# A fourth buffer for the scores of a top-16 retrieval, paid for from two other buffers

## The chip, the cores and the metric

The kernel runs on one core of a Trainium2 chip. The metric is the time of one execution on the device, in microseconds. Engines are named as in the profile: PE is TensorE (PEld its weight loads), DVE VectorE, ACT ScalarE, POOL GpSimd, SP SyncE, which issues most of the DMAs.

## What is computed

One layer of a hybrid of parallel branches, for a prompt of 1024 rows and a sample group of 64 rows that share all weights (D is 1024), in float32:

```
xn = rmsnorm(x);  p = xn @ w_in + b_in
x += (sum over 3 branches of sigmoid(gate) * branch(xn)) @ w_out     # mLSTM, spatial gating, cross-attention
xn = rmsnorm(x)                                                      # then the PEER experts:
q  = xn @ w_pq                                    # 8 heads x 256
s1, s2 = q[..., :128] @ k_sub1.T, q[..., 128:] @ k_sub2.T            # 128 scores each
(v1, i1), (v2, i2) = top16(s1), top16(s2)
cand = v1[:, None] + v2[None, :]                  # 16 x 16 candidates, again the top 16 of them
e, g = expert numbers, softmax of their scores    # 8 x 16 = 128 experts a row
a    = gelu(sum(u_exp[e] * xn));  x += sum((g * a) * v_exp[e])
y = rmsnorm(x)
```

There are 16384 experts. The outputs are y and the states of the branches.

## The kernel before

The rows are cut into nine tiles, 0 to 7 of 128 rows and "s" of 64, in three blocks: [0, 1], [2, 3, 4, "s"], [5, 6, 7]. Every float32 matmul is done as three products of a rounded part and a rest: a weight piece is loaded (`wraw`, L263), rounded by ScalarE (`wh`, L277), and its rest is formed by VectorE (`wl`, L280), for each use.

**Phase 1** runs `main` (the projections, block after block), `mlstm`, `side` (spatial gating and cross-attention), `retrieve`, `choose` and `experts` as streams. They are Python generators which yield planned costs; a small planner (`Flow`) interleaves their instructions into one program by these. The tile framework then lays out each engine's queue at build time, with its own simulation of times (`schedule_with_timeline_sim=True`): an instruction whose buffer isn't free there may be passed by a later one. [...]

`retrieve` goes, in each block, over four groups `g` of two heads and over the block's tiles: TensorE makes 4 x 128 scores (L819) into a PSUM buffer (`ms`, two of them, shared with transposes and branch work), ScalarE copies them, scaled, to `sc` (L822), and VectorE takes four top 16s of 128 scores (`top16`, L797 to L803: max, max_index, match_replace into the scratch `tk`, max, max_index). `sc` is last read by match_replace (L801), `tk` by the second max_index (L803). The buffers of `sc` have the tag `k4`, which `dk` and `gf` of phase 2 share. `choose` makes the 54 candidates of a head that can be in its top 16, takes their top 16 by the same `top16` with the same scratch, and decodes the expert numbers.

Rows then go two ways. Five tiles (0, 1, "s", 6, 7) gather their experts: GpSimd issues indirect DMAs (L1020) of one row of `u_exp` or `v_exp` per partition, three `gu` and four `gv` buffers; VectorE forms the products with xn (`gu`, L1033) and adds up the weighted v rows (`gacc` or `gx`, L1041, "a gacc" in short). Between a tile's u and v, `end_u` makes the weights `w2` of the v rows; the trace calls the tile `w`. The u of a tile alternate with the v of the tile before, u first.

Four tiles (2, 3, 4, 5) go the dense way, in **phase 2**, whose buffers take the memory of phase 1 (`first.close()`): all experts are computed for them. `ahead` loads xn (`dxn`), transposes it (`dxh`, `dxl`, L1135 to L1138) and does the first products with `u_exp` (`hidden`, L1114 to L1116); `dense` turns the chosen experts into a dense matrix of weights with one-hot products (L1192, L1196 on VectorE, L1205 on TensorE), stores it (`gd`), and then does the products with `v_exp` (L1263 to L1265) over all 16384 experts. "weights" is the signal that the dense matrix is done; `end_u` of tile "s" and the choice of tiles 6 and 7 wait for it by a one-element copy.

Of the kernel before, what the change touches and what calls it, by code (L numbers as in the profile page):

```python
# [7 lines left out]
F32 = mybir.dt.float32  # L8
# [57 lines left out]
def tile_stream_step(ctx: ExitStack, tc: tile.TileContext, a: dict, out: dict):  # L66
# [17 lines left out]
    gp = pool("gp", 1)  # L84
    kp = pool("kp", 1)
# [709 lines left out]
    NC = 54  # L795

    def top16(v, i, src, n):  # L797
        w = kp.tile([128, 128], F32, name="tk", bufs=4)[0:src.shape[0]]
        V.max(v[:, 0:8], src)
        V.max_index(i[:, 0:8], v[:, 0:8], src)  # L800
        V.match_replace(w[:, 0:n], v[:, 0:8], src, NEG)  # L801
        V.max(v[:, 8:16], w[:, 0:n])
        V.max_index(i[:, 8:16], v[:, 8:16], w[:, 0:n])  # L803

    def retrieve():
        for b, tiles in enumerate(BLOCKS):
            v16, i16 = {}, {}
            order = sorted(enumerate(tiles), key=lambda x: CHOOSE.index(x[1]))
            for g in range(4):
                yield f"pq{b}_{g}"  # L810
                pq = st.pop(("pq", b, g))
                for i, t in order:
                    L = ROWS_OF[t]
                    if g == 0:
                        v16[i] = kp.tile([128, 16, 16], F32, name="v16", bufs=NT)[0:L]
                        i16[i] = kp.tile([128, 16, 16], U16, name="i16", bufs=NT)[0:L]
                    p = ms()[0:L]
                    for c in range(4):
                        T.matmul(p[:, c * 128:(c + 1) * 128], pq[:, c, i * 128:i * 128 + L], ksub[:, c % 2, :],  # L819
                                 start=True, stop=True)  # L820
                    sc = kp.tile([128, 4, 128], F32, name="sc", tag="k4", bufs=3)[0:L]
                    S.activation(sc, p.rearrange("p (c k) -> p c k", c=4), AF.Copy, scale=st["r", b][0:L, i:i + 1])  # L822
                    yield 1.0
                    for c in range(4):
                        top16(v16[i][:, 4 * g + c, :], i16[i][:, 4 * g + c, :], sc[:, c, :], 128)
                        yield 1.1
                    if g == 3:
                        st["k", t] = v16[i], i16[i]
                        fl.signal(f"k{t}")
                fl.signal(f"sc{b}_{g}")  # L830
# [108 lines left out]
    def experts():  # L939
# [14 lines left out]
        def end_u(t):  # L954
            _, av = st_u.pop(t)
            e, gg = st.pop(("e", t))
            L = ROWS_OF[t]
            av, gg = av[:, 0:L], gg[:, 0:L]
            t1 = gp.tile([128, 128], F32, name="w2", bufs=2)[:, 0:L]
            if t == GT[2]:  # L960
                V.tensor_copy(t1[0:1, 0:1], st["weights"][0:1])
            S.activation(t1, av, AF.Square, scale=GELU_C ** 0.5)
            V.scalar_tensor_tensor(t1, t1, 1.0, av, op0=ALU.add, op1=ALU.mult)
            S.activation(t1, t1, AF.Tanh, scale=GELU_S)
            V.scalar_tensor_tensor(t1, t1, 1.0, av, op0=ALU.add, op1=ALU.mult)
            V.scalar_tensor_tensor(t1, t1, 0.5, gg, op0=ALU.mult, op1=ALU.mult)
            st_v[t] = (e, t1)
            fl.signal(f"u{t}")
# [176 lines left out]
    def dense():  # L1145
# [20 lines left out]
        for i, t in sorted(enumerate(DENSE), key=lambda x: CHOOSE.index(x[1])):  # L1166
            n = ROWS_OF[t]
            yield f"d{t}"
            k_ = kp.tile([128, 3, 128], F32, name="dk", tag="k4", bufs=3)[0:n]
            SP.dma_start(k_, dkd[t])  # L1170
            cs = slice(i * 128, i * 128 + n)
            p = two_banks()[:, 0, :]
            for j in range(3):
                T.transpose(p[:, j * 128:j * 128 + n], k_[:, j, :], ident[0:n, 0:n])
            S.copy(kb[:, :, cs], p.rearrange("p (s t) -> p s t", s=4)[:, 0:2, 0:n])
            gf = kp.tile([128, 128], F32, name="gf", tag="k4", bufs=3)
            S.copy(gb[:, 0, cs], p[:, 256:256 + n])
            V.tensor_tensor(gf[:, 0:n], p[:, 256:256 + n], gb[:, 0, cs], op=ALU.subtract)
            S.copy(gb[:, 1, cs], gf[:, 0:n])
            V.tensor_tensor(gb[:, 2, cs], gf[:, 0:n], gb[:, 1, cs], op=ALU.subtract)  # L1180
            V.tensor_copy(gf_[:, cs], gb[:, 2, cs])
            yield 3.0

            for t0 in range(i * 128, i * 128 + n, 32):
                sg = hp.tile([128, 32, 4, 32], F32, name="sg", bufs=2)
                for t1 in range(0, 32, 8):
                    p = two_banks()
                    for b in range(2):
                        tb = t0 + t1 + 4 * b
                        ts = slice(tb, tb + 4)  # L1190
                        eq, pr = hots[tb // 4 % len(hots)]
                        V.tensor_tensor(eq, io[:, None].to_broadcast([128, 2, 128, 4]),  # L1192
                                        kb[:, :, None, ts].to_broadcast([128, 2, 128, 4]), op=ALU.is_equal)

                        nd = 2 + b
                        V.tensor_tensor(pr[:, 0:nd], eq[:, 0, None].to_broadcast([128, nd, 128, 4]),  # L1196
                                        gb[:, 0:nd, None, ts].to_broadcast([128, nd, 128, 4]), op=ALU.mult)
                        for j in range(nd, 3):
                            for t2 in range(4):
                                S.activation(pr[:, j, :, t2], eq[:, 0, :, t2], AF.Copy,  # L1200
                                             scale=gf_[:, tb + t2:tb + t2 + 1])

                        for t2 in range(4):
                            for j in range(3):
                                T.matmul(p[:, b, t2 * 128:(t2 + 1) * 128], eq[:, 1, :, t2], pr[:, j, :, t2],  # L1205
                                         start=(j == 0), stop=(j == 2))
                        yield 0.4
                    S.copy(sg[:, :, :, t1:t1 + 8].rearrange("p g c t -> p (g c) t"),
                           p.rearrange("p b (t e) -> p e (b t)", t=4))
                    yield 0.4  # L1210
                nd1 += 32
                if nd1 == TD:
                    st["weights"] = tok = kp.tile([128, 1], F32, name="tok")
                    V.tensor_copy(tok, sg[:, 0, 0, 0:1])
                    fl.signal("weights")
                SP.dma_start(gd[:, :, t0 // 32].rearrange("g p c t -> p g (c t)"),
                             sg.rearrange("p g c t -> p g (c t)"))
# [5 lines left out]
        for i, t in enumerate(DENSE):  # L1223
            n = ROWS_OF[t]
# [19 lines left out]
        for g in range(NP // GP):  # L1244
            last = g == NP // GP - 1
            for j in range(2 * GP):
# [24 lines left out]
                if q == GP - 1:  # L1271
# [3 lines left out]
                    if last:  # L1275
                        if gfin is None:
                            gfin = gain(dp, "g_final", name="gfin", tag="ge", bufs=LG)
                        for i, t in enumerate(DENSE):
                            n = ROWS_OF[t]
# [88 lines left out]
```

## Time and profile before

| | |
|---|---|
| median of 3 runs | 3621.07 us (3614.02 to 3626.41) |
| the profiled execution | 3616.96 us, span 3615.1 us |
| busy: PE / DVE / POOL / ACT | 3267.5 / 3104.3 / 1616.1 / 1368.5 us |
| DMA | 1024.78 MB, 283 GB/s on average |
| instructions | 46206 |

Busy times are sums over a span in which several engines work at once. A line such as "L822 ACT ... sc<-ms,rn" names the source line, the engine, the tile written and the tiles read. A wait is put down to the instruction that ended it.

### The profile page before, as it was taken

The numbers are of one execution on the slowest core, as the hardware profiler recorded it, in microseconds if no ns is written. First come the engines' busy times: TensorE is split into PE (matmuls) and PEld (weight loads), VectorE is DVE, ScalarE is ACT, GpSimd is POOL, SyncE is SP. The second block draws the span as 40 slices with busy tenths as digits, with TensorE's granted clock in tenths as the row PEclk, the third lists the DMA queues.
The fourth block names the chain that finished last, engine by engine and source line by source line (L and its number), as shares of the span: only waits on it lengthen the run. The fifth ranks groups of instructions, "written<-read, shape, count | busy, mean of one in ns | idle before, by whom it ended". The sixth has DMA issues, their size and how long they took to land.

```text
span 3615.1 us, 46206 instructions
## 1 busy us (share of the span) xinstructions
PE 3267.5 (90%) x15364; PEld 2637.6 (73%) x15364; DVE 3104.3 (86%) x6493; ACT 1368.5 (38%) x2479; POOL 1616.1 (45%) x1208
## 2 busy tenths in 40 slices
PE   8999899899997496798949786999999999999998
PEld 7787876576677374586847785888778888887886
DVE  5555697778999999899999998998779888888998
ACT  5555534333333243333424673333223333332332
POOL 1000324446654776455422304664446455544654
PEclk9999999899999698898969797999999999999999
DMA  7455567789998787898876758999889999988997
GB/s 236 149 166 180 163 217 265 254 277 328 336 365 299 268 309 261 259 346 291 302 232 197 221 175 287 344 351 329 293 295 383 337 339 339 342 311 299 385 345 262
DMA packets 447436, 1024.78 MB, mean 283 GB/s; under 512 B 32182, under 2 KB 169566, under 8 KB 443100
## 3 DMA queue, kind: packets, MB, share of 16 engines
q0 software_dynamic: 166528, 604.58, 47.4%
q1 hardware_dynamic: 276828, 413.06, 33.7%
q10 hardware_dynamic: 3840, 4.20, 0.3%
q8 instruction: 120, 1.97, 0.2%
q14 instruction: 120, 0.98, 0.1%
HBM read 968.44 MB, written 53.26 MB: 283 GB/s over the span
## 4 chain that ended last, share of the span: by engine, by line
PE 59%; DVE 16%; issue 10%; DMA 9%; POOL 5%; ACT 1%; SPq 0%; POOLq 0%; DVEq 0%; ACTq 0%
DMA gu<-in_u_exp_dram,e 5%; PE ph L1116 5%; PE ph L1114 5%; PE ph L1115 5%; PE po L1265 5%; PE po L1263 5%; PE po L1264 5%; PE acc L311 5%; PE acc L312 5%; PE acc L313 4%; POOL gu L1020 4%; PE po L1205 3%; DVE gu L1033 3%; DVE gacc L1041 3%; PE acc L328 2%
## 5 line engine op out<-in xcount | busy, mean ns | idle before, releaser
L277 ACT CAST wh<-wraw 128x512 fp32r<-128x512 f32 x994 | 612.8, 621 | 1339.8 <-PE ph L1115 455.2
L1020 POOL DMA_INDIRECT gv<-in_v_exp_dram,e x522 | 739.0, 1416 | 804.7 <-DVE gacc L1041 346.1
L1020 POOL DMA_INDIRECT gu<-in_u_exp_dram,e x576 | 753.3, 1308 | 746.4 <-DVE gu L1033 494.0
L280 DVE TENSOR_TENSOR wl<-wraw,wh 128x512 fp32r<-128x512 f32 x962 | 652.7, 684 | 219.1 <-ACT wh L277 215.0
L1033 DVE SCALAR_TENSOR_TENSOR gu<-gu,gx 128x1024 f32<-128x1024 f32 x576 | 699.9, 1217 | 141.9 <-DMA gu<-in_u_exp_dram,e 139.9
L1041 DVE SCALAR_TENSOR_TENSOR gacc<-gv,w,gacc 128x1024 f32<-128x1024 f32 x448 | 570.9, 1274 | 9.0 <-DMA gv<-in_v_exp_dram,e 8.8
L312 PE MATMUL acc<-wl,half 128*128 128x512 f32 (+1 forms) x1152 | 473.2, 411 | 1.0 <-DVE wl L280 1.0
L313 PE MATMUL acc<-wh,half 128*128 128x512 f32 (+1 forms) x1152 | 455.9, 401 | 0.0
L1263 PE MATMUL po<-wh,W 128*128 128x512 f32 x1024 | 399.5, 398 | 30.7 <-ACT W L1233 30.1
L311 PE MATMUL acc<-wh,half 128*128 128x512 f32 (+1 forms) x1152 | 411.3, 409 | 6.2 <-ACT uB L470 4.7
L1264 PE MATMUL po<-wl,W 128*128 128x512 f32 x1024 | 407.8, 398 | 4.3 <-DVE wl L280 4.3
L1116 PE MATMUL ph<-dxh,wl 128*128 128x512 f32 x1024 | 403.0, 394 | 7.7 <-DVE wl L280 7.7
L1265 PE MATMUL po<-wh,W 128*128 128x512 f32 x1024 | 407.4, 398 | 0.6 <-DVE W L1234 0.6
L1114 PE MATMUL ph<-dxh,wh 128*128 128x512 f32 x1024 | 401.6, 392 | 1.3 <-DVE dxl L1138 1.3
L1115 PE MATMUL ph<-dxl,wh 128*128 128x512 f32 x1024 | 401.1, 392 | 0.0
L328 PE MATMUL acc<-half,wh 128*128 128x256 f32 (+2 forms) x768 | 251.8, 347 | 16.7 <-ACT wh L277 12.1
L311 PEld LDWEIGHTS acc<-wh,half 128*128 128x128 f32 (+1 forms) x1152 | 210.3, 183 | 76.7 <-issue 14.9
L329 PE MATMUL acc<-half,wh 128*128 128x256 f32 (+2 forms) x768 | 260.9, 344 | 0.4 <-DVE half L232 0.4
L312 PEld LDWEIGHTS acc<-wl,half 128*128 128x128 f32 (+1 forms) x1152 | 211.6, 184 | 65.6 <-issue 12.7
L1263 PEld LDWEIGHTS po<-wh,W 128*128 128x128 f32 x1024 | 193.9, 189 | 78.0 <-issue 31.7
L313 PEld LDWEIGHTS acc<-wh,half 128*128 128x128 f32 (+1 forms) x1152 | 210.6, 184 | 54.2 <-issue 1.9
L330 PE MATMUL acc<-half,wl 128*128 128x256 f32 (+2 forms) x768 | 230.0, 345 | 15.3 <-DVE wl L280 10.4
(447 smaller groups left out, 5056.2 us busy)
## 6 DMA issues: line engine op xcount, KB each, us to landing
wraw<-in_w_in_dram SPq DMA_DIRECT2D x216, 512.0 KB
wraw<-in_v_exp_dram SPq DMA_DIRECT2D x126, 512.0 KB
wraw<-in_u_exp_t_dram SPq DMA_DIRECT2D x67, 512.0 KB
gd<-sg SPq DMA_DIRECT2D x16, 2048.0 KB
g<-gd SPq DMA_DIRECT2D x32, 1024.0 KB
wrawx<-in_u_exp_t_dram SPq DMA_DIRECT2D x61, 512.0 KB
wraw<-in_w_pq_dram SPq DMA_DIRECT2D x48, 512.0 KB
wraw<-in_w_out_dram SPq DMA_DIRECT2D x24, 512.0 KB
```

The costliest lines, as they stand in the source:

```text
L277: S.copy(h, t)
L280: E.tensor_tensor(l, t, h.bitcast(F32), op=ALU.subtract)
L311: T.matmul(ps[i], xh[:, cs], h, start=(k == 0), stop=False)
L312: T.matmul(ps[i], xh[:, cs], l, start=False, stop=False)
L313: T.matmul(ps[i], xl[:, cs], h, start=False, stop=(last and b is None))
L1020: G.indirect_dma_start(out=tl, out_offset=None, in_=src, in_offset=bass.IndirectOffsetOnAxis(ap=col, axis=0))
L1033: V.scalar_tensor_tensor(tl, tl, 1.0, xn, op0=ALU.mult, op1=ALU.mult, accum_out=av[:, j:j + 1])
L1041: V.scalar_tensor_tensor(x2, gt_.pop(op), st_v[t][1][:, j:j + 1], x2, op0=ALU.mult, op1=ALU.add)
L1116: T.matmul(o, l[:, cs], xh[:, k + kk, :], start=False, stop=(k + kk == KD - 1))
L1263: T.matmul(o, hi, h, start=(q == 0 and k == 0), stop=False)
L1264: T.matmul(o, hi, l, start=False, stop=False)
L1265: T.matmul(o, lo, h, start=False, stop=(q == GP - 1 and k == 1))
```

## The change

The scores get four buffers for three, in all three places that use the tag `k4`; the scratch of the top 16 gets two for four, and `w2` one for two. In bytes per partition: 2048 more, 2 x 512 and 512 less. The program is otherwise the same, instruction for instruction.

```diff
     def top16(v, i, src, n):
-        w = kp.tile([128, 128], F32, name="tk", bufs=4)[0:src.shape[0]]
+        w = kp.tile([128, 128], F32, name="tk", bufs=2)[0:src.shape[0]]
...
-                    sc = kp.tile([128, 4, 128], F32, name="sc", tag="k4", bufs=3)[0:L]
+                    sc = kp.tile([128, 4, 128], F32, name="sc", tag="k4", bufs=4)[0:L]
...
-            t1 = gp.tile([128, 128], F32, name="w2", bufs=2)[:, 0:L]
+            t1 = gp.tile([128, 128], F32, name="w2", bufs=1)[:, 0:L]
...
-            k_ = kp.tile([128, 3, 128], F32, name="dk", tag="k4", bufs=3)[0:n]
+            k_ = kp.tile([128, 3, 128], F32, name="dk", tag="k4", bufs=4)[0:n]
...
-            gf = kp.tile([128, 128], F32, name="gf", tag="k4", bufs=3)
+            gf = kp.tile([128, 128], F32, name="gf", tag="k4", bufs=4)
```

## Rows read from the trace of the kernel before

**Rows 1.** The page's head: the span, and busy time, share of the span and number of instructions of each engine.

```profile
span 3615.1 us, 46206 instructions
...
PE 3267.5 (90%) x15364; PEld 2637.6 (73%) x15364; DVE 3104.3 (86%) x6493; ACT 1368.5 (38%) x2479; POOL 1616.1 (45%) x1208
```

**Rows 2.** Waits by engine: engine and line that waited, what it waited for, us in total, times, the longest in us. The first three over the whole span, the last in the stretch from 1150 to 1300 us.

```profile
ACT sc L822 <- DVE tk L801: 103.4, 14, 15.3
...
PE ms L819 <- ACT sc L822: 65.7, 8, 15.7
...
PE ms L225 <- ACT sc L822: 10.8, 1, 10.8
...
ACT sc L822 <- DVE tk L801: 57.0, 8, 15.3
```

**Rows 3.** Busy time by stage: the stretch in us from the span's start and its length, busy us and (instructions) of each engine, the granted clock of PE as a share of full speed, the share of the DMA engines, GB/s.

```profile
1150.00:1290.00 140.00, 74.92 (x352) 65.36 (x351) 134.03 (x444) 34.18 (x61) 95.66 (x61) 0.72 0.78 263
1290.00:1400.00 110.00, 110.00 (x470) 82.67 (x470) 106.12 (x323) 48.70 (x90) 75.65 (x44) 1.00 0.86 303
1400.00:1480.00 80.00, 33.41 (x104) 21.38 (x103) 72.35 (x255) 20.91 (x50) 43.28 (x31) 0.62 0.73 241
1480.00:1820.00 340.00, 317.56 (x1476) 262.99 (x1475) 325.21 (x759) 132.11 (x257) 161.39 (x120) 0.95 0.88 302
1820.00:1890.00 70.00, 22.69 (x119) 21.01 (x117) 70.00 (x286) 10.75 (x18) 23.36 (x24) 0.63 0.69 215
1890.00:2182.00 292.00, 250.61 (x1820) 230.25 (x1820) 272.16 (x587) 181.43 (x372) 60.54 (x32) 0.87 0.65 203
2182.00:2216.00 34.00, 4.28 (x9) 2.98 (x10) 26.85 (x74) 6.06 (x7) 9.87 (x9) 0.51 0.89 300
2216.00:3608.00 1392.00, 1371.16 (x5896) 1110.64 (x5894) 1231.83 (x1696) 429.37 (x638) 741.98 (x563) 0.99 0.92 330
```

**Rows 4.** ScalarE's timeline, the copies of the scores in block 1 and at the end of block 2: start in us, duration in us, engine, line, operation, tiles, and in brackets the idle time before it and what ended that.

```profile
1155.16 0.69 ACT L822 ACTIVATE sc<-ms,rn 128x512 f32<-128x512 f32 x1 [2.20 <-DVE tk L801]
...
1170.73 0.68 ACT L822 ACTIVATE sc<-ms,rn 64x512 f32<-64x512 f32 x1 [12.82 <-DVE tk L801]
1183.60 0.69 ACT L822 ACTIVATE sc<-ms,rn 128x512 f32<-128x512 f32 x1 [12.18 <-DVE tk L801]
...
1200.17 0.69 ACT L822 ACTIVATE sc<-ms,rn 128x512 f32<-128x512 f32 x1 [5.08 <-DVE tk L801]
...
1867.61 0.69 ACT L822 ACTIVATE sc<-ms,rn 128x512 f32<-128x512 f32 x1 [7.57 <-DVE tk L801]
1876.32 0.69 ACT L822 ACTIVATE sc<-ms,rn 128x512 f32<-128x512 f32 x1 [8.03 <-DVE tk L801]
1884.58 0.69 ACT L822 ACTIVATE sc<-ms,rn 128x512 f32<-128x512 f32 x1 [7.57 <-DVE tk L801]
```

**Rows 5.** VectorE's timeline at the end of block 2's retrieval, from one step to the next. FIND_INDEX8 and MATCH_REPLACE8 are the max_index and match_replace of the code.

```profile
1876.13 1.27 DVE L1041 SCALAR_TENSOR_TENSOR gacc<-gv,w,gacc 128x1024 f32<-128x1024 f32 x1
1877.32 0.86 DVE L802 MAX8 v<-tk 128x8 f32<-128x128 f32 x4
...
1878.88 1.25 DVE L1041 SCALAR_TENSOR_TENSOR gacc<-gv,w,gacc 128x1024 f32<-128x1024 f32 x1
...
1880.66 0.28 DVE L803 FIND_INDEX8 i<-v,tk 128x8 uint16<-128x128 f32 x1
...
1880.92 0.28 DVE L803 FIND_INDEX8 i<-v,tk 128x8 uint16<-128x128 f32 x1
...
1882.16 1.26 DVE L1041 SCALAR_TENSOR_TENSOR gacc<-gv,w,gacc 128x1024 f32<-128x1024 f32 x1
...
1883.42 0.27 DVE L801 MATCH_REPLACE8 tk<-v,sc 128x128 f32<-128x128 f32 x1
...
1884.20 0.27 DVE L801 MATCH_REPLACE8 tk<-v,sc 128x128 f32<-128x128 f32 x1
1884.39 1.27 DVE L1041 SCALAR_TENSOR_TENSOR gacc<-gv,w,gacc 128x1024 f32<-128x1024 f32 x1
```

**Rows 6.** The hand-over to phase 2: the first DMA issues of SP and the first matmuls of PE in it.

```profile
1885.30 1.99 SPq L1131 DMA_DIRECT2D dxn<-xn2d  x4
...
1891.63 1.94 PE L1135 MATMUL ph<-ident,dxn 128*128 128x128 f32 x8 [21.21 <-DMA dxn<-xn2d]
```

**Rows 7.** VectorE's timeline, two interleaved chains of the decoding of expert numbers (L879 and L880 add to one half of `xy`, each L883 to the other; L889 reads all of `xy`).

```profile
2190.51 0.21 DVE L879 TENSOR_TENSOR xy<-xy,pq__18811 128x128 bf16<-128x128 bf16 x1
2190.64 0.28 DVE L883 SCALAR_TENSOR_TENSOR xy<-pq__18811,xy 128x128 bf16<-128x128 bf16 x1
2190.85 0.21 DVE L880 TENSOR_TENSOR xy<-xy,pq__18811 128x128 bf16<-128x128 bf16 x1
2190.98 0.28 DVE L883 SCALAR_TENSOR_TENSOR xy<-pq__18811,xy 128x128 bf16<-128x128 bf16 x1
2191.29 1.43 DVE L889 SCALAR_TENSOR_TENSOR oh<-xy,ib 128x256 bf16<-128x256 bf16 x4
```

**Rows 8.** What the dense weights release: the timelines of POOL and of PE behind them; and the last gaccs of tile 7 that read `gv` (duration in ns min/median/max, first and last start).

```profile
2182.53 0.94 POOL L1020 DMA_INDIRECT gv<-in_v_exp_dram,e  x1 [104.37 <-DVE tk L801]
...
2211.14 0.77 PE L1263 MATMUL po<-wh,W 128*128 128x512 f32 x1 [30.12 <-ACT W L1233]
...
L1041 DVE SCALAR_TENSOR_TENSOR gx<-gv,w,gx x74: 1271/1279/1324, 3321.3 to 3595.1; 128x1024 f32<-128x1024 f32 x74
```

## Prediction

> **What bounds the kernel now.** I read the page first, then the stages, then the waits on the tiles that the change touches. By busy time alone TensorE (90%) is the bound and VectorE (86%) comes next [rows 1]. The table by stage says where each is true [rows 3]. From 2216 us on TensorE is busy 1371.16 of 1392 us: a stretch bound by TensorE. Between 1150 and 2182 us it is VectorE that is full: 134.03 of 140 us while block 1 is retrieved, 72.35 of 80 us around 1400 us, 70.00 of 70 us at the end of block 2's retrieval, 272.16 of 292 us while the dense weights are made, and in the first of these TensorE does 74.92 us of work in 140, in the third 22.69 in 70, at 0.63 of its clock.
>
> The waits name the tiles [rows 2]. ScalarE's copy of the scores (`sc`, L822) waits 103.4 us in 14 waits for the match_replace of a top 16 (L801), the last reader of a score buffer. TensorE in turn waits for that copy: 65.7 us before the score matmuls and 10.8 us before a transpose which needs the same PSUM buffers, 76.5 us in all. The copies go in steps: 13 to 17 us apart in block 1, 8.3 to 8.7 us in block 2 [rows 4]. One step on VectorE, from one gacc at 1876.13 to the like one at 1884.39, is 8.26 us: three gacc of about 1.19 us from start to start (3.57 us) and four chains of a top 16 (4.69 us) with no idle time [rows 5]. The three score buffers thus don't starve VectorE. They only keep ScalarE and TensorE from running further ahead of it.
>
> Two points are passed by everything. The second phase starts when the last score copy (1884.58 plus 0.69 us) has given back the memory of the first: the loads of `dxn` go out at 1885.30, TensorE resumes at 1891.63 [rows 6]. And the dense weights, done at about 2182 us, release the gathers, for which GpSimd has stood 104.37 us, and TensorE's second product, after 30.12 us of idling [rows 8]. What follows takes 3615.1 - 2182 = 1433 us, and the experts' last gacc starts at about 3595 [rows 8], so both chains behind that point end nearly together. **A microsecond counts if the weights come earlier by it, or if a chain behind them gets shorter.**
>
> **The change part by part.** No instruction and no DMA is added or removed; buffers change, and with them what may run ahead, and the order which the planner writes for each queue.
>
> *Fourth buffer, at the end of block 2.* Copy n waits for the release of copy n-4 in place of n-3, so the last copy may go when the copy before it goes now: 1876.32 for 1884.58, -8.26 us [rows 4].
>
> *Scratch of the top 16 from four to two.* Now four match_replaces (L801) come in a row and then the score buffer is free [rows 5]. With two scratch tiles, chains 3 and 4 can't write theirs before L802 and L803 of chains 1 and 2 have read theirs. That puts two L802 (0.20 us each from start to start) and two L803 (0.26 us each) ahead of the release: 0.92 us if they follow at once. If the planner lets a gacc in at each of the two turns, as it does at each turn now, it is 0.92 + 2 x 1.19 = 3.3 us. I take one gacc, 2.1 us. Below nothing it can't go: the release can't move ahead of its own readers. Above, a whole further step, 8.26 us, if the halves of a tile fall into different steps. Net for the last copy: -6.2 us, bounds -7.3 and 0.
>
> *Order of dependent instructions.* Two chains are interleaved, not four, so an instruction may follow the one it depends on more closely. Two interleaved chains of small operations show what that costs: an L883 that reads the result of the L883 before it, with one L880 of the other chain between, starts without a gap, and all of them overlap their neighbours by about 0.08 us. Only L889, which follows its producer directly, starts 0.31 us after it, 0.11 us more than such an operation otherwise takes [rows 7]. Chains in pairs have one instruction between, so I take nothing. Upper bound: three turns in each pair, 72 pairs of score chains and 36 of candidates, 324 x 0.11 = 36 us, nearly all of it in front of 2182 us.
>
> *How much of the 6.2 us reaches the weights.* From 1890 to 2182 us VectorE has 20 us idle and TensorE 41 [rows 3]. An earlier start saves only what comes out of VectorE's 20 us: the top 16s left over at the hand-over (now one tile more) are work of the same engine. The gacc would be displaced freely, for GpSimd stands still for 104 us before the weights, but they share VectorE too. I take half, -3 us; bounds 0 and -7.3.
>
> *Fourth buffer, in block 1.* One step is 13 us (1170.73 to 1183.60), less 2 to 6 us for the scratch, as steps here are longer: TensorE would enter block 2 some 9 us earlier. From 1290 to 1400 us it is full; from 1400 to 1480 us it works 33.41 us of 80 while VectorE is at 72.35 [rows 3]. So TensorE runs 9 us ahead into a wall that VectorE sets. I take -2 us, bounds 0 and -9.
> In block 0 nothing: 8 of the 14 waits lie in block 1 [rows 2], the other six are block 2's steps of 8.3 to 8.7 us.
>
> *One buffer for the gathered weights `w2`.* A tile's `w2` may be written only when the last gacc of the tile before has read its own. The last u comes just ahead of that gacc in the order, so each of four turnovers waits for one gacc, 1.27 us [rows 5], and its gather. Two lie before the weights, under GpSimd's 104 us. Two lie behind them, 2.5 us in all, in a chain whose last gacc starts 20 us before the end [rows 8]. I take nothing; bound +5.
>
> *`dk` and `gf`* share the ring of `sc`: the first load of `dk` can go a step earlier, together with the hand-over. Nothing of its own.
>
> Sum: -3 - 2 = -5 us. The profiled execution took 3616.96 us (span 3615.1), 4.1 us under the median of 3621.07. So 3616.96 - 5 = 3612 in its terms, and **3616 us** as a median. Anything within 0.3%, 11 us, can hardly be told from no change on this kernel.
>
> [...]
>
> **The rivals.**
> - *Both gains last* (0.23). The 6 to 7 us at the hand-over and 9 to 13 us of block 1 reach the weights whole, -15 to -20: 3601 to 3606. For it: 20 us of VectorE idle between 1890 and 2182, and about 8 and 15 us before, between 1400 and 1820 [rows 3]. Against it: that is all there is to take.
> - *All 76.5 us of stalls go* (0.03): 3621 - 76 = 3545. [...] Against it: VectorE is full in them. [...]
> - *The scratch becomes the gate* (0.22), the slower side. Place: match_replace of chains 3 and 4. If between the halves of a tile a step's worth of gacc gets in, the release comes 8.26 us later, which eats the fourth buffer; from that point on each step gets longer. With half the 36 us of dependent turns, or 1.2 to 2.4 us for each of some 10 full steps, it is +12 to +24: 3633 to 3645. For it: gacc at every turn now [rows 5]. Against it: VectorE's work stays the same and gacc done early are not done later.
> - *The change is hidden, but the queues come out in another order* (0.10), which can go either way. The nearest row is the stall between 1400 and 1480 us, 46 us of TensorE. I take up to 20: 3601 or 3641.
>
> **How the numbers follow.** Forecast: within 11 us of before, at -5, chance 0.42; its own range is 3610 to 3626. Faster by over 0.3%: 0.23 + 0.03 + 0.05 = 0.31. Slower: 0.22 + 0.05 = 0.27. The range leaves out the 0.03, a few hundredths of the reordering and the upper part of the slower rival: 3594 to 3641.
>
> **What would show it.** Right: the copies L822 in block 1 and 2 one step earlier against L801, the loads of `dxn` 4 to 8 us before 1885, TensorE's wait on `sc` shorter by some 20 us, the weights 1 to 7 us before 2182, and VectorE still full from 1150 to 1290. L801 in twos. The stretch behind the weights still 1430 us. Wrong: `dxn` at 1885 or later (the scratch gates), the weights 15 us or more ahead (VectorE was not the wall), or a change behind the weights (`w2`, or another order).

## The result, and the profile after

The changed kernel takes 3655.03 us (median of 4 executions, 3643.14 to 3661.83), the kernel before 3623.74 beside it: ratio 1.0071, 95% interval 1.0049 to 1.0094. The medians lie 31 us apart, the ratio stands for 26 us. The time is outside the range of the prediction, on the side of its slower rival and beyond that rival's 3633 to 3645 us too. The profiled executions, the quickest of the changed kernel's four and a quick one of the kernel before, stand 26.3 us apart, 3641.4 for 3615.1 us of span [rows 1].

The page's head of the changed kernel:

```profile
span 3641.4 us, 46213 instructions
...
PE 3258.4 (89%) x15364; PEld 2628.0 (72%) x15364; DVE 3109.4 (85%) x6493; ACT 1359.4 (37%) x2475; POOL 1588.5 (44%) x1208
```

VectorE is busy 5 us longer than before and the other engines less long, for the same numbers of matmuls and VectorE instructions: the loss is nearly all idle time. The timelines of SP, POOL and PE at the two points that everything passes, the hand-over and the weights:

```profile
1935.54 1.75 SPq L1131 DMA_DIRECT2D dxn<-xn2d  x4
...
2208.96 2.04 POOL L1020 DMA_INDIRECT gv<-in_v_exp_dram,e  x1 [271.77 <-DVE tk L801]
...
2236.55 0.77 PE L1263 MATMUL po<-wh,W 128*128 128x512 f32 x1 [28.49 <-ACT W L1233]
```

`dxn` is loaded 50.2 us later (1885.30 in [rows 6]), the weights are done 26.4 us later (POOL at 2182.53, PE at 2211.14 in [rows 8]), and behind them nothing changed: 3641.4 - 2209.1 = 1432.3 us, before 1433.0. So the whole loss lies ahead of the weights, and nearly half of the delay at the hand-over is won back between the two. GpSimd now stands for 271.77 us before the weights; before it was 104.37. ("The weights" are the last store of the dense matrix, at 2209.1 us here and 2182.1 us before.)

Busy time by stage, cut at each kernel's own hand-over and weights (columns as in [rows 3]); the kernel before:

```profile
1150.00:1885.30 735.30, 558.59 (x2514) 453.40 (x2512) 703.01 (x2041) 246.65 (x475) 395.85 (x274) 0.85 0.82 280
1885.30:2182.10 296.80, 250.61 (x1820) 230.25 (x1820) 276.96 (x608) 181.51 (x373) 64.03 (x35) 0.87 0.66 205
```

and the changed one:

```profile
1150.00:1935.50 785.50, 547.28 (x2474) 444.26 (x2472) 740.55 (x2045) 238.90 (x468) 424.25 (x306) 0.83 0.84 286
1935.50:2209.10 273.60, 250.40 (x1820) 231.52 (x1820) 237.82 (x561) 177.65 (x369) 1.75 (x2) 0.91 0.50 150
```

Ahead of the hand-over VectorE (the third busy time) does 37.5 us more, behind it 39.1 us less. POOL's count behind it tells what moved: 35 gathers before, 2 now. The gaccs of tile 1 that were done there are now done ahead of the hand-over. Groups of VectorE from 1000 us to the hand-over, and from there to the weights (count, busy us and mean ns), before:

```profile
L1041 DVE SCALAR_TENSOR_TENSOR gacc<-gv,w,gacc 128x1024 f32<-128x1024 f32 x182 | 231.3, 1271 | 4.8 <-DMA gv<-in_v_exp_dram,e 4.7
L1041 DVE SCALAR_TENSOR_TENSOR gacc<-gv,w,gacc 128x1024 f32<-128x1024 f32 x35 | 44.6, 1275 | 0.0
```

after:

```profile
L1041 DVE SCALAR_TENSOR_TENSOR gacc<-gv,w,gacc 128x1024 f32<-128x1024 f32 x215 | 274.8, 1278 | 2.5 <-DMA gv<-in_v_exp_dram,e 1.7 <-DMA gacc<-x2d 0.7
L1041 DVE SCALAR_TENSOR_TENSOR gacc<-gv,w,gacc 128x1024 f32<-128x1024 f32 x2 | 2.5, 1275 | 0.0
```

33 gaccs changed sides; at 1.19 us from start to start [rows 5] they are 39 of the 50 us. VectorE's idle time makes the rest of the sum: from 1150 us to the hand-over it went from 32.3 to 45.0 us, from there to the weights from 19.8 to 35.8, together 28.6 us, about what the weights are late. Behind the hand-over TensorE has 250 us of work in both kernels and is idle 23 us in the changed one, 4.2 of them the end of a wait of 14.8 us for `dxn`, so that of its 273.6 us little is left to be saved; VectorE now waits there, 20 us for ScalarE and 13 us for TensorE.

Where the 33 got in: the same groups of VectorE from 1000 us to the last copy of block 1 (1286.3 us before, 1353.3 us after), and from the first copy of block 2 (1796.4 and 1809.9 us) to the hand-over. Before:

```profile
L1041 DVE SCALAR_TENSOR_TENSOR gacc<-gv,w,gacc 128x1024 f32<-128x1024 f32 x59 | 75.0, 1271 | 0.1
L1041 DVE SCALAR_TENSOR_TENSOR gacc<-gv,w,gacc 128x1024 f32<-128x1024 f32 x25 | 31.7, 1267 | 0.0
```

after:

```profile
L1041 DVE SCALAR_TENSOR_TENSOR gacc<-gv,w,gacc 128x1024 f32<-128x1024 f32 x81 | 103.8, 1282 | 0.0
L1041 DVE SCALAR_TENSOR_TENSOR gacc<-gv,w,gacc 128x1024 f32<-128x1024 f32 x36 | 45.9, 1276 | 1.5 <-DMA gv<-in_v_exp_dram,e 1.5
```

So 22 got in while block 1 was retrieved and 11 in block 2; between the blocks there are 98 in both. The 22 are gaccs of tile 0 (its last ones come at about 1387 us, before at about 1433), which stand ahead of the hand-over in any case. But the gaccs then run 22 ahead, keep that lead, and so 22 more of tile 1 come in ahead of the hand-over.

How they got in: the copies of the scores (ScalarE's timeline, block 1 and block 2), as in [rows 4]:

```profile
1185.41 0.69 ACT L822 ACTIVATE sc<-ms,rn 128x512 f32<-128x512 f32 x1 [22.48 <-DVE tk L801]
...
1264.19 0.68 ACT L822 ACTIVATE sc<-ms,rn 64x512 f32<-64x512 f32 x1 [23.49 <-DVE tk L801]
1290.71 0.69 ACT L822 ACTIVATE sc<-ms,rn 128x512 f32<-128x512 f32 x1 [25.84 <-DVE tk L801]
...
1809.94 1.30 ACT L822 ACTIVATE sc<-ms,rn 128x512 f32<-128x512 f32 x2
...
1817.57 0.69 ACT L822 ACTIVATE sc<-ms,rn 128x512 f32<-128x512 f32 x1 [0.20 <-PE ms L819]
...
1863.36 0.69 ACT L822 ACTIVATE sc<-ms,rn 128x512 f32<-128x512 f32 x1 [8.82 <-DVE tk L801]
1878.96 0.69 ACT L822 ACTIVATE sc<-ms,rn 128x512 f32<-128x512 f32 x1 [14.92 <-DVE tk L801]
1894.09 0.69 ACT L822 ACTIVATE sc<-ms,rn 128x512 f32<-128x512 f32 x1 [14.44 <-DVE tk L801]
1908.69 0.69 ACT L822 ACTIVATE sc<-ms,rn 128x512 f32<-128x512 f32 x1 [13.91 <-DVE tk L801]
...
1934.82 0.69 ACT L822 ACTIVATE sc<-ms,rn 128x512 f32<-128x512 f32 x1 [6.49 <-DVE tk L801]
```

and before, the first copies of block 2:

```profile
1796.43 1.27 ACT L822 ACTIVATE sc<-ms,rn 128x512 f32<-128x512 f32 x2 [0.39 <-DVE rn L200]
```

They are 25 to 33 us apart at the end of block 1 (before 13 to 22). In block 2 the first four go into the four buffers, the next comes only 45.8 us later, while VectorE does 15 gaccs and decodes a tile of block 1; then come three steps of 15 us (before 8.3 to 8.7), and the last four go 5 to 8 us apart, with three gaccs left among them. From its first copy to the hand-over block 2 takes 125.6 us, for 88.9 before, which is 37 of the 50 us. VectorE does 34 us more there, 14 of it the 11 gaccs and most of the rest the decoding of that tile, of which before nearly nothing was left when block 2 began. The other 13.5 us, by which block 2 starts later, are not shown to belong to the change: of the kernels below, e2, e10 and e12 retrieve as before and start it at 1806.0 to 1809.3 us.

The waits over the whole span (columns as in [rows 2]):

```profile
ACT sc L822 <- DVE tk L801: 147.1, 11, 25.8
...
PE ms L819 <- ACT sc L822: 143.9, 10, 26.3
```

ScalarE's wait, 103.4 us before [rows 2], was to shrink with a fourth buffer; it grew, and TensorE's more than doubled. VectorE's timeline in one step of block 2 shows why (to be read beside [rows 5]):

```profile
1878.84 1.28 DVE L1041 SCALAR_TENSOR_TENSOR gacc<-gv,w,gacc 128x1024 f32<-128x1024 f32 x1
1880.03 0.30 DVE L802 MAX8 v<-tk 128x8 f32<-128x128 f32 x1
1880.24 0.75 DVE L889 SCALAR_TENSOR_TENSOR oh<-xy,ib 128x256 bf16<-128x256 bf16 x2
...
1881.87 1.27 DVE L1041 SCALAR_TENSOR_TENSOR gacc<-gv,w,gacc 128x1024 f32<-128x1024 f32 x1
...
1884.97 1.27 DVE L1041 SCALAR_TENSOR_TENSOR gacc<-gv,w,gacc 128x1024 f32<-128x1024 f32 x1
...
1886.22 0.28 DVE L801 MATCH_REPLACE8 tk<-v,sc 128x128 f32<-128x128 f32 x1
...
1887.55 1.28 DVE L1041 SCALAR_TENSOR_TENSOR gacc<-gv,w,gacc 128x1024 f32<-128x1024 f32 x1
...
1889.81 1.27 DVE L1041 SCALAR_TENSOR_TENSOR gacc<-gv,w,gacc 128x1024 f32<-128x1024 f32 x1
...
1891.87 1.27 DVE L1041 SCALAR_TENSOR_TENSOR gacc<-gv,w,gacc 128x1024 f32<-128x1024 f32 x1
...
1893.91 1.28 DVE L1041 SCALAR_TENSOR_TENSOR gacc<-gv,w,gacc 128x1024 f32<-128x1024 f32 x1
```

A step lasts from 1878.84 to 1893.91, 15.07 us, where it was 8.26. With four scratch tiles the four chains of a tile move together through their stages, with a gacc at each of three turns. With two they move in two halves, so there are six turns, and a gacc stands at each: six in place of three, 7.1 us in place of 3.6. Small operations of the decoding of another tile (L889, L892, L896, L897) stand between them too, 3.2 us. The four chains themselves still take 4.7 us. 4.7 + 7.1 + 3.2 = 15.0.

### The profile page after: what moved, and what is told of

It reads as the page before. It is cut to its first block, busy times and chain, and to the rows that moved or that the text cites. A ratio compares the mean times of both kernels' runs of the same rounds, so it can differ in the third digit from the quotient of the medians.

```text
span 3641.4 us, 46213 instructions
## 1 busy us (share of the span) xinstructions
PE 3258.4 (89%) x15364; PEld 2628.0 (72%) x15364; DVE 3109.4 (85%) x6493; ACT 1359.4 (37%) x2475; POOL 1588.5 (44%) x1208
## 4 chain that ended last, share of the span: by engine, by line
PE 61%; DVE 13%; issue 11%; DMA 9%; POOL 4%; ACT 1%; DVEq 0%; SPq 0%; POOLq 0%; ACTq 0%
DMA gu<-in_u_exp_dram,e 6%; PE acc L311 6%; PE acc L312 6%; PE acc L313 6%; PE po L1265 5%; PE po L1264 5%; PE po L1263 5%; PE ph L1114 5%; PE ph L1116 5%; PE ph L1115 5%; PE po L1205 5%; POOL gu L1020 4%; DVE gacc L1041 3%; DVE gu L1033 2%; DVE wl L280 1%
## 5 line engine op out<-in xcount | busy, mean ns | idle before, releaser
L1020 POOL DMA_INDIRECT gu<-in_u_exp_dram,e x576 | 731.1, 1269 | 716.9 <-DVE gu L1033 468.2
L313 PE MATMUL acc<-wh,half 128*128 128x512 f32 (+1 forms) x1152 | 457.5, 403 | 0.0
L311 PE MATMUL acc<-wh,half 128*128 128x512 f32 (+1 forms) x1152 | 420.6, 413 | 6.4 <-ACT uB L470 5.1
L328 PE MATMUL acc<-half,wh 128*128 128x256 f32 (+2 forms) x768 | 249.4, 343 | 16.1 <-ACT wh L277 12.4
L329 PE MATMUL acc<-half,wh 128*128 128x256 f32 (+2 forms) x768 | 255.5, 339 | 0.0
```

Source lines behind the costliest of these rows:

```text
L311: T.matmul(ps[i], xh[:, cs], h, start=(k == 0), stop=False)
L313: T.matmul(ps[i], xl[:, cs], h, start=False, stop=(last and b is None))
L1020: G.indirect_dma_start(out=tl, out_offset=None, in_=src, in_offset=bass.IndirectOffsetOnAxis(ap=col, axis=0))
```

## The experiments

The theory to be tested: the scratch gates, and what it costs is the other work that gets in at its turns ahead of the hand-over. Against it stood `w2`, the order of the queues, and block 1. Hand-overs, weights and gaccs are read from one profiled execution of each kernel, the ratios and their 95% intervals from all executions.

**One part at a time.** e1 takes only the scratch, e2 only `w2`.

```diff
-        w = kp.tile([128, 128], F32, name="tk", bufs=4)[0:src.shape[0]]
+        w = kp.tile([128, 128], F32, name="tk", bufs=2)[0:src.shape[0]]
```

> The scratch of the top 16 has two tiles, the scores keep three buffers and w2 two: one part of the change alone. Theory S (the scratch gates: chains 3 and 4 of a tile wait for chains 1 and 2, and a gacc gets in at each of twice as many turns): the steps of the score copies at the end of block 2 are 14 to 16 us as in the changed kernel (8.3 before), the loads of dxn go out at 1935 us or later, and the time is 3640 to 3670 us. Theory F (the fourth score buffer does harm by another order of TensorE's and ScalarE's queues) and theory W (one buffer for w2 does it): steps of 8 to 9 us, dxn near 1885 us, time as before, 3614 to 3630 us.

```diff
-            t1 = gp.tile([128, 128], F32, name="w2", bufs=2)[:, 0:L]
+            t1 = gp.tile([128, 128], F32, name="w2", bufs=1)[:, 0:L]
```

> Only w2 has one buffer for two; scores and scratch as before. Theory W: the turnover of w2 costs the 26 to 31 us, 3640 us or more. Theories S and F: at most two turnovers of a gacc behind the dense weights, 0 to 5 us, so 3614 to 3630 us.

Measured: e1 1.0074 [1.0047, 1.0102] (3656.66 us), hand-over 1953.8, weights 2224.0: the scratch alone is the whole loss. In the profiles the changed kernel has its hand-over 18 us earlier than e1, which would be the rest of the change; in the medians, 3655.03 and 3656.66 us, none of that shows. e2 1.0019 [0.9999, 1.0039] (3634.2 us, above the 3614 to 3630 expected), hand-over 1895.8: not told apart from nothing, nor from a few us.

**The fourth buffer without its price.** It fits beside four scratch tiles if two small tiles share a buffer (`pos` and `ggd`), `r1` is formed in place and `w2` has one buffer. e4 makes these savings alone, e3 adds the fourth buffer.

```diff
-        pos = kp.tile([128, 8, 16], U32, name="pos", bufs=1)[0:L]
+        pos = kp.tile([128, 8, 16], U32, name="pos", tag="pg", bufs=1)[0:L]
...
-        gg = kp.tile([128, 8, 16], F32, name="ggd")[0:L]
+        gg = kp.tile([128, 8, 16], F32, name="ggd", tag="pg", bufs=1)[0:L]
...
-        q = kp.tile([128, 6, 128], BF, name="pq_")[0:L]
+        q = kp.tile([128, 5, 128], BF, name="pq_")[0:L]
...
+        r1 = yf
```

> Four score buffers, the scratch keeps its four tiles, w2 has one. The room comes from the decoding of the expert numbers: the positions and the softmax terms share one buffer, and one of six rows of small scratch is formed in place. Theory S: nothing gates any more, the last score copy goes one step of 8.3 us earlier, dxn at 1875 to 1880 us, and the time is between that of the control (e4) and 8 us below it, 3606 to 3628 us. Theory F: 3640 us or more with four scratch tiles too.

> Control for e3: three score buffers and four scratch tiles as before, w2 with one buffer, and the same saving in the decoding of the expert numbers as e3. All theories: steps of 8 to 9 us, dxn near 1885 us, 3614 to 3630 us. If it is off by over 11 us, the planner's other order for the queues is by itself as large as what is looked for.

Measured: e3 1.0012 [0.9996, 1.0028], e4 1.0022 [1.0008, 1.0036]. Against its control the hand-over of e3 is 5.7 us earlier (1891.2 for 1896.9, where 1875 to 1880 was expected) and the weights are 5.0 us later (2200.2 for 2195.2). Both are less than kernels with one and the same retrieval differ by, and the medians (3631.83 for 3635.47 us) don't stand apart beyond the scatter either. So no gain of the fourth buffer is shown, and none of some us is excluded. e4 is 0.2% slower than the kernel before, where nothing was expected; e2, which shares only the one buffer of `w2` with it, has nearly as much, and whether that is `w2` or another order of the queues stays open.

**The dose.** Three scratch tiles (e5) and six (e6, with three score buffers and the savings).

> Three scratch tiles, all else as before (three score buffers, two of w2): the dose between four and two. Theory S with turns (a scratch tile is held for three turns, L801, L802, L803, and a gacc gets in at each; so a score tile of four chains takes 12/n turns with n scratch tiles: 3, 4, 6 for n = 4, 3, 2): a step at the end of block 2 is 4.69 + 4 x 1.19 = 9.5 us where no other work gets in, the loads of dxn go out 8 to 20 us after those of before, and the time is a third of the way from before to e1, 3630 to 3642 us. Rival (a threshold: two tiles are too few for latency, three are enough): as before, within 6 us.

> Six scratch tiles, three score buffers, two of w2; the room comes from the small buffers of the decoding as in e4. Theory S with turns: 12/6 = 2 turns, a step of 4.69 + 2 x 1.19 = 7.1 us if the score buffers allow it, the loads of dxn 5 to 15 us earlier than in e4, and the time 3 to 10 us under e4, 3625 to 3633 us. Rival (four scratch tiles cover all, the score buffers set the step): steps of 8 to 9 us, 3630 to 3640 us as e4.

Measured: e5 1.0076 [1.0053, 1.0099], as bad as two, where a third of it was expected. VectorE's timeline of e5:

```profile
1888.19 1.27 DVE L1041 SCALAR_TENSOR_TENSOR gacc<-gv,w,gacc 128x1024 f32<-128x1024 f32 x1
...
1889.45 0.28 DVE L801 MATCH_REPLACE8 tk<-v,sc 128x128 f32<-128x128 f32 x1
...
1890.16 1.28 DVE L1041 SCALAR_TENSOR_TENSOR gacc<-gv,w,gacc 128x1024 f32<-128x1024 f32 x1
1891.35 0.68 DVE L802 MAX8 v<-tk 128x8 f32<-128x128 f32 x3
...
1892.72 1.26 DVE L1041 SCALAR_TENSOR_TENSOR gacc<-gv,w,gacc 128x1024 f32<-128x1024 f32 x1
```

The chains go in threes, three turns for three chains and a gacc at each, so four turns for a tile, as expected. The steps of block 2 from 1854.4 to 1934.3 us are 10.0 us on average (9.5 expected), and block 2 takes 104.8 us to the hand-over, 16 more than before. Up to here the dose holds. But block 2 starts at 1830.2 us, 21 to 24 us later than in e2, e10 and e12, with 70 gaccs done by the end of block 1 (59 before); e1 is as late, 1837.3, the changed kernel with its fourth buffer isn't (1809.9). What delays that start is not shown, and by it the forecast of the time fell. e6 1.0066 [1.004, 1.0092] (3644 us, for 3625 to 3633 expected): the hand-over came 14 us earlier than in e4 (1882.9), as expected, but the weights 13 us later (2208.3). So it isn't "a later hand-over is worse"; an earlier one is worse as well.

**Without the gaccs.** e7 is the kernel before and e8 the changed one, both without 126 of the 128 v rows of tile 1 (neither gathered nor added).

```diff
+                if t == 1 and 0 < j < 127:
+                    gt_[op] = None
+                    cnt[kind] += 1
+                    return
                 col = st_v[t][0][:, j:j + 1]
...
+            if gt_[op] is None:
+                gt_.pop(op)
+                cnt["v"] -= 1
+                return
             V.scalar_tensor_tensor(x2, gt_.pop(op), st_v[t][1][:, j:j + 1], x2, op0=ALU.mult, op1=ALU.add)
```

> The kernel before, but 126 of the 128 rows of v of tile 1 are left out, gathers and gaccs: no gacc can get in at the turns of block 2's retrieval. Pair with e8; it is their difference that counts. All theories: steps at the end of block 2 about 4.7 us, plus what the decoding of tile 4 takes; dxn 20 us or more before 1885 us.

> The changed kernel with the same 126 rows of v of tile 1 left out. Theory S with turns (the gacc that gets in at each of six turns is the price): without gaccs the steps at the end of block 2 are like those of e7 within 1.5 us, and of the 50 us by which the loads of dxn went out later only what block 1 adds is left, at most 25 us. Rival (the price is the latency of dependent instructions in pairs): steps 3 us or more longer than in e7.

Measured, one execution each: e7 3530.95, e8 3516.97 us. The 14 us are within what two executions of one kernel differ by; what counts is that the changed kernel is no longer the slower one, and that its hand-over comes at 1811.9 us, for 1824.6 in e7. Copies in block 2, and the stretch from its first copy to the hand-over (columns as in [rows 3]), e7 and then e8:

```profile
1796.59 0.69 ACT L822 ACTIVATE sc<-ms,rn 128x512 f32<-128x512 f32 x1 [0.45 <-PE ms L819]
1805.21 0.69 ACT L822 ACTIVATE sc<-ms,rn 128x512 f32<-128x512 f32 x1 [0.45 <-PE ms L819]
1810.97 0.69 ACT L822 ACTIVATE sc<-ms,rn 128x512 f32<-128x512 f32 x1 [0.45 <-PE ms L819]
...
1767.06:1824.60 57.54, 56.17 (x351) 55.79 (x349) 56.77 (x314) 27.48 (x47) 0.00 (x0) 1.00 0.33 105
```

```profile
1783.86 0.69 ACT L822 ACTIVATE sc<-ms,rn 128x512 f32<-128x512 f32 x1 [0.45 <-PE ms L819]
1792.47 0.69 ACT L822 ACTIVATE sc<-ms,rn 128x512 f32<-128x512 f32 x1 [0.45 <-PE ms L819]
1798.23 0.69 ACT L822 ACTIVATE sc<-ms,rn 128x512 f32<-128x512 f32 x1 [0.45 <-PE ms L819]
...
1754.32:1811.90 57.58, 56.18 (x351) 55.79 (x349) 56.80 (x314) 27.46 (x47) 0.00 (x0) 1.00 0.33 108
```

The same steps of 8.6 and 5.8 us (4.7 had been expected), 57.5 and 57.6 us in all with TensorE and VectorE both full, and in both the copies wait for TensorE, no longer for a match_replace. So where no gacc can get in, two scratch tiles cost nothing in block 2, and the rival (latency) falls. In block 1 of e8 the copies are still 24 to 32 us apart (e7 13 to 23), among the gaccs of tile 0, which are left in; yet its block 2 doesn't start later (1754.3 us, e7 1767.1). So the longer retrieval of block 1 is no delay by itself. It costs through the lead of 22 gaccs that it gives, once there are gaccs of tile 1 to come in by it: the loss needs the gaccs.

**The gaccs back on their side.** In e9 and e10 the last 35 gaccs of tile 1 wait for the weights, in the changed kernel and in the one before; in e12 the last 11 (row 117 for 93).

```diff
+                if ops[nxt] == ("v", GT[1], 93):
+                    yield "weights"
                 issue(ops[nxt])
...
+            if op == ("v", GT[1], 93):
+                V.tensor_copy(tl[0:1, 0:1], st["weights"][0:1])
             G.indirect_dma_start(out=tl, out_offset=None, in_=src,
```

> The changed kernel, in which the last 35 gaccs of tile 1 are made to wait for the dense weights (a one-element copy of the weights' token into the buffer that the gather of row 93 fills, as the kernel already does elsewhere). Counted from 1000 us on, the kernel before had done 182 gaccs when dxn was loaded at 1885.3 and 35 more until the weights at 2182.1; the changed kernel 215 by 1935.5 and 2 until 2209.1. Theory (it is the 33 gaccs that got in ahead of the hand-over, not the scratch itself): 182 gaccs ahead again, so dxn 33 x 1.27 = 42 us earlier, 1893 (1885 to 1900), though the scratch still has two tiles; with no gacc behind it the dense stretch stays at the 270 to 274 us of the runs that had 2 or fewer there, so the weights at 2160 to 2170. If the 35 held gaccs fit into the time in which VectorE is idle behind the weights (228 us of 1491), the end follows: span 3590 to 3610. Rival A (two scratch tiles cost by themselves, through turns and waits): dxn at 1915 or later. Rival B (the experts' chain sets the end too): the held gaccs come back at the end, up to 35 x 1.27 = 44 us, span 3630 to 3650.

> The kernel before with the same hold of the last 35 gaccs of tile 1. Theory: nothing changes ahead of the hand-over (182 gaccs, dxn at 1885 within 5 us); behind it no gacc is left, so the dense stretch goes from 296.8 to 265 to 274 us and the weights come at 2150 to 2160; if the held gaccs find room behind the weights the span is 3585 to 3600 and the kernel beats both, by 0.4 to 0.8%. Rival B: the gaccs held lengthen the experts' chain, span 3615 to 3635. Rival C (the dense stretch is TensorE's own and VectorE's gaccs in it cost nothing): stretch still 290 to 297 us, the weights at 2180.

Measured ahead of the weights: e9 has 181 gaccs ahead of the hand-over, which comes at 1903.4 in place of 1935.5, with the two scratch tiles unchanged; the weights come at 2177.7, ahead of the kernel before. e10, with 181 as well, has its hand-over at 1893.7. So of the changed kernel's delay 32 us go with the gaccs, and rival A (1915 or later) falls. About 10 us between e9 and e10 are left to the rest of the change: VectorE waits 33.4 us for gathered u in e9 and 17.8 in e10, and the medians, too, are 9.4 us apart (3648.90 and 3639.49). The forecasts were missed by 3 to 4 us for both hand-overs and by 8 us for both weights. In e10 the dense stretch falls from 296.8 to 274.7 us:

```profile
1893.70:2168.40 274.70, 248.15 (x1820) 229.46 (x1820) 235.34 (x565) 178.13 (x369) 6.51 (x5) 0.91 0.52 156
```

But the end doesn't follow: e9 1.006 [1.0034, 1.0085], e10 1.0034 [1.0016, 1.0053], as rival B had it (2 us beyond its span for e10, 3637.3). The room of 228 us in which the held gaccs were to fit was counted to 3700 us, 59 us past the end of the changed kernel; up to the end VectorE is idle 170 us of 1432. The last matmul and the last gacc of e10:

```profile
3572.78 0.40 PE L1269 MATMUL po<-wh,W 128*128 128x512 f32 x1
...
3627.21 1.28 DVE L1043 SCALAR_TENSOR_TENSOR gx<-gv,w,gx 128x1024 f32<-128x1024 f32 x1 [0.25 <-DMA gv<-in_v_exp_dram,e]
```

TensorE's last matmul starts 27 us earlier than before (3599.3), the experts' chain's last gacc 32 us later than at 3595.1 [rows 8]: the held gaccs come back there, 35 x 1.27 = 44 us, less the 14 us by which the weights are earlier.

> The kernel before with a hold of the last 11 gaccs of tile 1 only, in place of 35. With 35 held, TensorE's last matmul started at 3572.3 in place of 3598.9, but the experts' chain ended 65 us behind it, 1469 us after the weights; without a hold it ends some 12 us ahead of TensorE's. Theory (three limits, of which the kernel before stands near the balance): 24 gaccs are left in the dense stretch, which loses 11 of 35 parts of 22 us, 7 us, so it is 288 to 292 us long; the experts' chain gets 11 x 1.27 = 14 us longer, about as much as its slack; both chains end together, 3606 to 3614 where the hand-over stays at 1885, plus what the order of the queues shifts it (8 us with 35 held): ratio 0.998 to 1.002. Rival (a smaller hold is free): ratio 0.993 to 0.997.

Measured: 0.9991 [0.9977, 1.0004], the dense stretch 282.9 us, the weights 2181.1. No gain, as forecast, and no loss. The stretch fell by more than forecast (288 to 292), while the hand-over (1898.2) and the span of the profiled execution (3629.0) lay above it.

**No scratch and four buffers.** e11 is the changed kernel, but writes the scores back in place, and `w2` has two buffers again.

```diff
-        w = kp.tile([128, 128], F32, name="tk", bufs=2)[0:src.shape[0]]
+        w = src
...
-            t1 = gp.tile([128, 128], F32, name="w2", bufs=1)[:, 0:L]
+            t1 = gp.tile([128, 128], F32, name="w2", bufs=2)[:, 0:L]
```

> Four score buffers and no scratch at all: match_replace writes the scores back into their own buffer, w2 stays at two. No chain can wait for a scratch tile; a score buffer is then free after the last max_index (L803) of its tile instead of the last match_replace (L801), some 2 us later. In the queue as built, 186 gaccs of 256 stand ahead of the hand-over, against 225 in the kernel before and 256 in the changed one. Theory (the number of gaccs ahead sets the hand-over, those behind it lengthen the dense stretch): dxn at 1840 to 1865, 33 to 39 gaccs earlier; 70 gaccs in the dense stretch, which gets 330 to 350 us long (54 gaccs made it 325); the weights at 2180 to 2205, ratio 1.000 to 1.006. Rival (fewer buffer waits are a gain wherever they are): weights 20 us or more ahead of 2182, ratio under 0.995.

Measured: 1.0049 [1.0029, 1.007]. TensorE's waits on the copies, and its dense stretch:

```profile
PE ms L225 <- ACT sc L822: 4.4, 1, 4.4
PE ms L819 <- ACT sc L822: 2.1, 2, 1.5
```

```profile
1869.00:2210.10 341.10, 255.02 (x1820) 229.32 (x1820) 320.42 (x669) 180.51 (x371) 161.18 (x72) 0.76 0.74 234
```

Of the 76.5 us of TensorE's stalls 6.5 are left, the hand-over comes 16 us earlier, and the kernel is slower: 71 gaccs now stand behind the hand-over, and the weights come at 2210.1. The stretch and the ratio are as expected; the hand-over and the weights lie 4 and 5 us above their bounds.

All kernels together, from their profiled executions (gaccs counted from 1000 us on):

| kernel | gaccs ahead | hand-over | gaccs behind, to the weights | stretch between | weights |
|---|---|---|---|---|---|
| e11 in place | 147 | 1869.0 | 71 | 341.1 | 2210.1 |
| e6 six scratch | 163 | 1882.9 | 54 | 325.4 | 2208.3 |
| e3 | 179 | 1891.2 | 41 | 309.0 | 2200.2 |
| e4 | 183 | 1896.9 | 36 | 298.3 | 2195.2 |
| before | 182 | 1885.3 | 35 | 296.8 | 2182.1 |
| e2 | 183 | 1895.8 | 33 | 295.6 | 2191.4 |
| e12, 11 held | 182 | 1898.2 | 23 | 282.9 | 2181.1 |
| e5 three scratch | 208 | 1935.0 | 10 | 278.2 | 2213.2 |
| after | 215 | 1935.5 | 2 | 273.6 | 2209.1 |
| e1 two scratch | 216 | 1953.8 | 2 | 270.2 | 2224.0 |
| e10, 35 held | 181 | 1893.7 | 0 | 274.7 | 2168.4 |
| e9, 35 held | 181 | 1903.4 | 0 | 274.3 | 2177.7 |

Prices can be estimated from pairs of these profiles. Behind the hand-over a gacc costs about (341.1 - 278.2) / 61 = 1.03 us (e11 against e5), but below ten the stretch hardly gets shorter (278.2 at ten, 270 to 275 at two or none), with 250 us of it TensorE's work. Ahead of it, it costs 1.21 us between e4 and the changed kernel (38.6 us for 32), 1.5 from the kernel before (50.2 for 33). The kernel before lies in the valley between them, and behind the weights the experts' chain and TensorE end nearly together: no place was found to which gaccs could be moved at a gain. No version here beats it.

## Why the prediction was wrong

- **What bounds the kernel: right.** The hand-over and the weights decide; behind them 1432.3 us for 1433.0.
- **The step that failed is the scratch's term.** The prediction saw a gacc at every turn [rows 5] and took 2.1 us for the release of one score buffer, added once, to the last copy. Two things were wrong. The turns: a tile has six for three, so three more gaccs in a step, not one, and the decoding of another tile falls into the step as well, 6.8 us in all (15.07 for 8.26). And the number of times: VectorE is full (idle 2.4 of the 125.6 us that block 2 takes to the hand-over), so what gets in lengthens the steps wherever there are gaccs, not only the last release: three steps of block 2, and block 1, whose steps went from 13 to 22 us to 25 to 33. Eleven more gaccs than before lie between the first copy of block 2 and the hand-over (36 for 25), 22 more in block 1, 33 in all.
- **"gacc done early are not done later" was the reason to give the slower rival only 0.22.** It holds for work, not for time: 39.1 us left the dense stretch, and it got 23.2 us shorter. The row that says so was there: TensorE works 250.61 of the 292 us [rows 3], which leaves about 41 us at most to be saved, and only the 20 us in which VectorE was idle were taken as a limit. Of the 39 us moved, 16 came back as idle time of VectorE (35.8 for 19.8). The rival had the place, the sign and "each step gets longer"; its +12 to +24 was too little, with 1.2 to 2.4 us a step where 6.8 were measured.
- **The fourth buffer: its worth is not shown.** -8.26 us alone was forecast for the hand-over, and half of the net to reach the weights. e3 against e4 has -5.7 us at the hand-over and +5.0 at the weights, neither clear of the scatter. The direction fits e6 and e11: there, too, an earlier hand-over has fewer gaccs ahead of it, and they reappear behind it.
- **Dependents closer together cost nothing: borne out** where it could be seen alone, by the equal steps of e7 and e8 (8.6 and 5.8 us in both). **`w2`, nothing: not refuted**, e2 is 0.2% slower with an interval that reaches from nothing to 0.4%. **Block 1, -2 us: wrong**, the retrieval ends 67 us later there (1353 for 1286). e8 shows that this is no delay by itself; what it brings is 22 of the 33 gaccs.
- **Taking the stalls away gained nothing.** e11 takes 70 of TensorE's 76.5 us of stalls away and is 0.5% slower all the same; the engine that was full at the end of block 2's retrieval was VectorE (70.00 of 70 us [rows 3]), not TensorE, which had the gaps (22.69 of 70 us). From 1150 us to the weights, too, VectorE was the busiest engine (980 of 1032 us before, TensorE 809), and e7, which takes 126 gaccs off it (and their gathers off GpSimd and the DMA engines), is 86 us faster than the profiled execution before; e7 leaves this work out, so it shows the worth of VectorE's time and no way to get it.
- **The sign that was named, `dxn` at 1885 or later, appeared**, 50 us late. Its reading, the scratch gates, was right.

## What to carry to other kernels

Where an engine's queue is laid out at build time, a turn of a chain of dependent instructions needn't be idle time but can be a place for other ready work (here a gacc at each of six turns, 7.1 us of a step of 15.07, on an engine without idle time in it). To take buffers from such a chain adds turns (here two tiles for four made six of three) and so moves other work ahead of whatever waits for the chain: count the turns for each item, times what fills one, times all the items, and follow how far ahead the other work then runs. And before work that changes sides of a border is counted as neutral, look at every engine's work in the stretch that it leaves: that stretch gets no shorter than the next engine's own work (here 273.6 us with 250.4 us of TensorE's).

## What the runs showed of the chip that was not expected

- TensorE's mean granted clock in the dense stretch was lower in the kernels with more gaccs there: 0.91 to 0.94 of full speed with two or none (after, e8, e10), 0.89 with 23 (e12), 0.87 with 35 (before), 0.79 with 54 (e6), 0.76 with 71 (e11), for the same 1820 matmuls. TensorE stood idle more in these: 23 us of the stretch in the changed kernel, 46 before, 86 in e11, of which 10, 25 and 58 us were waits for VectorE's one-hot tiles. Its busy time moved only from 246 us (e8) to 255 us (e11). So of the 63 us by which the stretch is longer in e11 than in e5 at most 4 are TensorE's own busy time (255.0 for 251.4); the rest is waiting.
- One kernel's executions differ more than one would like: the kernel before took 3612.4 to 3640.6 us, and its profiled execution (3616.96) is one of the quick ones. Kernels with the same retrieval and nearly the same gaccs ahead had the hand-over between 1893.7 and 1898.2 (e2, e4, e10, e12), before at 1885.3. Differences of 10 us between two profiles are not read as causes here.
